# Three mixed pairs of contraction tiles in ten gate/up units of each layer, in another order, with the residual in DRAM meanwhile

## The chip, the cores and the metric

One core of one Trainium2 chip runs the whole program. The metric is the device time of one execution in microseconds. The program is built from instructions for five engines, each with its own in-order queue: TensorE (PE) multiplies, VectorE (DVE) and ScalarE (ACT) work elementwise, GpSimd (POOL) and SyncE (SP) here mostly issue transfers and small steps. Semaphores order them.

## The reference

256 tokens of width 2048 pass two layers: a Mamba-2 layer, then a sliding-window attention layer. Each has a SwiGLU feed-forward part, and around every part stands an RMS norm on both sides. The change concerns the feed-forward part alone:

```python
D_MODEL, SEQ, DEPTH = 2048, 256, 2
D_FF = 5632

def swiglu(u, w_gate, w_up, w_down):
    return (jax.nn.silu(u @ w_gate) * (u @ w_up)) @ w_down

for layer in range(DEPTH):
    g = norm_w[layer]
    mix = mamba2_mixer(...) if layer == 0 else sliding_window_sink_attention(...)
    h = h + rmsnorm(mix, g[1])
    ffn = swiglu(rmsnorm(h, g[2]), ffn_w_gate[layer], ffn_w_up[layer], ffn_w_down[layer])
    h = h + rmsnorm(ffn, g[3])
```

All data are float32.

## The kernel before

**Products.** A float32 product is made of three matmuls in a rounded format: high half by high half, high by low, low by high. ScalarE casts a weight tile to its high half (`whi`, L114), VectorE subtracts that from the weight for the low half (`wlo`, L115). The activations `xh`, `xl` are split once per part. The contraction of 2048 is cut into 16 tiles of 128, and the class `Weights` walks through the weights of the whole program in a fixed list of specs.

**Weight rings.** A raw tile is 128 x 1024 float32: two contraction tiles of 512 columns, 512 KB, one transfer on SP's queue (L70). There are `RAWB` = 5 raw buffers. A sub-tile is what is converted at once; there are `CVB` = 4 buffers each for `whi` and `wlo`, so the conversion of a sub-tile waits for TensorE to be through with the fourth one before it. Loads run four raw tiles ahead, conversions three sub-tiles.

**Units.** The gate and up products of a layer run over 11 units of 512 columns. A *plain* unit takes 8 sub-tiles of gate (`G0` to `G7` below) and 8 of up (`U0` to `U7`), each of two contraction tiles: 2 token halves x 2 tiles x 3 = 12 matmuls of 128 x 512, 192 in the unit. In a *mixed* unit some pairs (e, o) of contraction tiles are multiplied for gate and up together by seven products in place of eight: the 2 x 2 scheme has the token halves and the two contraction tiles on one side, and gate and up of both tiles on the other. Such a pair takes two raw tiles, `ta` = gate(e), up(o) and `tb` = gate(o), up(e), each loaded by two transfers of 256 KB, and four sub-tiles, named "a" (`ta` itself), "13" (sums of `ta` and up(e), L87), "24" (two more sums, L90 and L91, each of 128 x 512) and "g" (gate(o) alone, 128 x 512). The seven products make 21 matmuls in place of 24. The matching sums of the activations, `sx`, are made once a layer by `mixed_x`. The products are summed over all pairs in seven banks p1 to p7 and one more, `up1`; behind the last pair and at the end of the unit VectorE puts them together (L700 to L703, L708), ScalarE applies silu, and VectorE multiplies gate and up (L712). `store_half` transposes a half of the previous unit's result on TensorE (4 transposes, L644) and splits it into `hh` and `hl` (L237 on ScalarE, L238 on VectorE).

Before the change units 1 to 8 are mixed, with `SPAIRS` = 2 pairs each (186 matmuls); units 0, 9 and 10 are plain. `S_ORDER` is [0, 2, 1, 3, 4, 5, 6, 7]: numbers below `SPAIRS` are mixed pairs, the others are plain pairs of contraction tiles, gate then up. The two store halves stand after positions 5 and 6.

**What sets the order.** The instructions are issued in program order on each engine, with a scheduler that moves what the code marks as urgent. So VectorE's queue holds the low halves, the sums of weights, the sums of banks and the splitting of the stores in one fixed order, and each waits behind the one ahead of it.

**Space.** `h`, the residual, is 128 x 2 x 2048 float32 in SBUF for the whole program (L469 on). In the feed-forward part `hh` and `hl` of units 0 to 7 lie in one pair of tiles, and those of units 8 to 10 in another (`Cat`, `late`) that takes the place of `sx`, `vh`, `t13` and `t24` when the mixed units are over.

**Entry.** In unit 0, `a_first` updates `h` by the mixer's result chunk by chunk (L533) while it makes the gate product. Then `row_factor` takes the norm's row factors from `h` (L223, L224, and a power on POOL, L228), and `mixed_x` is called between the sub-tiles of up 0.

Of the kernel before, what the change touches and what calls it, by code (L numbers as in the profile page):

```python
# [14 lines left out]
P = 128  # L15
# [15 lines left out]
SPAIRS = 2  # L31
S_FIRST, S_LAST = 1, 8
LATE = 8


class Weights:
# [40 lines left out]
    def _mixed(self, i, part):  # L77
# [11 lines left out]
        t24 = self.spool.tile([P, 2, CW], F32, tag="t24", name="t24")  # L89
        nc.vector.tensor_tensor(t24[:, 0, :], self.t13[:, 0, :], ta[:, 1, :], add)  # L90
        nc.vector.tensor_tensor(t24[:, 1, :], t24[:, 0, :], tb[:, 0, :], add)  # L91
        return t24[:]
# [42 lines left out]
def tile_yoco(ctx: ExitStack, tc: tile.TileContext, a: dict):  # L135
# [11 lines left out]

    rest = list(range(SPAIRS, KD // SUB))
    S_ORDER = [i for n in range(SPAIRS) for i in ([n] + rest[n : n + 1])][: 2 * SPAIRS - 1] + rest[SPAIRS - 1 :]
    S_END = S_ORDER.index(SPAIRS - 1)  # L150

# [320 lines left out]
    h = hpool.tile([P, NT, D], F32, tag="h", name="h")  # L472
    for t in range(NT):
        nc.sync.dma_start(h[:, t, :], x[P * t : P * (t + 1), :])
# [55 lines left out]
    def add_residual(mix, t, c):  # L530
        bks, rs = mix
        hs = h[:, t, CW * c : CW * (c + 1)]
        nc.vector.scalar_tensor_tensor(hs, bks[c][t][:], rs[t][:, 0:1], hs, ALU.mult, ALU.add)  # L533

    def a_first(key, mix, g, xt):
# [11 lines left out]
        def step(c, t):  # L547
            with tc.high_priority():
                update(c, t)
                to_xt(h[:, t, CW * c : CW * (c + 1)], t, c, g, xt)  # L550
# [24 lines left out]
    def row_factor():  # L575

        return [norm_stats(hpool, h, t) for t in range(NT)]
# [17 lines left out]
    class Cat:  # L595


        def __init__(self, n, early, late):
            self.n, self.tiles = n, (early, late)

        def at(self, k0, k1, ts):
            t = k0 >= self.n
            return self.tiles[t][:, k0 - self.n * t : k1 - self.n * t, ts]

        def __getitem__(self, idx):
            _, kt, ts = idx
            return self.at(kt, kt + 1, ts)[:, 0, :]

    def ffn(layer, mix):
        xt = new_xt()  # L610
        xh, xl, _ = xt
        with tc.tile_pool(name="ffn%d" % layer, bufs=1, side="right") as fp:
            early = [fp.tile([P, 4 * LATE, T], F32R, tag=n, name=n) for n in ("hh", "hl")]
            spool = tc.tile_pool(name="mixed%d" % layer, bufs=1, side="right")
            W.spool = sp = spool.__enter__()
            sx = sp.tile([P, SPAIRS, 4, 2, P], F32R, tag="sx", name="sx")
            vh = sp.tile([P, 2, CW], F32, tag="vh", name="vh")
            hid = None
# [9 lines left out]
            def mixed_x(i):  # L628


                y = sp.tile([P, 2, T], F32, tag="sy", name="sy")
                ks = slice(SUB * i, SUB * i + 2)
                nc.vector.tensor_tensor(y[:], xh[:, ks, :].bitcast(F32), xl[:, ks, :].bitcast(F32), ALU.add)
                e0, e1, o0, o1 = y[:, 0, :P], y[:, 0, P:], y[:, 1, :P], y[:, 1, P:]
                f = sp.tile([P, 4, P], F32, tag="sf", name="sf")
                for n, p, q in ((1, e1, o1), (3, e0, e1), (2, e0, f[:, 1, :]), (0, o0, f[:, 2, :])):
                    nc.vector.tensor_tensor(f[:, n, :], p, q, ALU.subtract)
                split_bank(sx[:, i, :, 0, :], sx[:, i, :, 1, :], f[:])

            def store_half(u, t):  # L640

                pt = bank()
                for k in range(4):
                    nc.tensor.transpose(pt[:, P * k : P * (k + 1)], scr[:, NT + t, P * k : P * (k + 1)], ident[:])  # L644
                ts = slice(P * t, P * (t + 1))
                split_bank(hid[0].at(4 * u, 4 * u + 4, ts), hid[1].at(4 * u, 4 * u + 4, ts),
                           pt[:].rearrange("p (k t) -> p k t", k=4))
# [5 lines left out]
            def mixed_unit(u):  # L653
# [28 lines left out]
                for pos, i in enumerate(S_ORDER):  # L682
                    e, o = SUB * i, SUB * i + 1
                    if i < SPAIRS:
                        for part, prods in (("a", (("p1", raw_x(e, 0)), ("p3", form(i, 0)))),
                                            ("13", (("p5", form(i, 1)), ("p7", form(i, 3)))),
                                            ("24", (("p6", form(i, 2)), ("p4", raw_x(o, 1)))),
# [16 lines left out]
                    if pos in (5, 6):  # L704
                        store_half(u - 1, pos - 5)
# [10 lines left out]
            for u in range(FF // CW):  # L716
                if S_FIRST <= u <= S_LAST:
                    if u == S_FIRST:
                        hid = [Cat(4 * LATE, e, None) for e in early]
                    mixed_unit(u)  # L720
                    if u == S_LAST:
                        spool.__exit__(None, None, None)
                        lpool = tc.tile_pool(name="late%d" % layer, bufs=1, side="right")
# [523 lines left out]
```

## Time and profile before

| | us |
|---|---|
| median of 3 runs | 2410.99 |
| lowest, highest run | 2410.32, 2412.8 |
| profiled execution, its own time | 2411.38 |
| its span | 2409.7 |
| TensorE busy | 2390.0 |
| TensorE weight loads busy | 1980.7 |
| VectorE busy | 1667.9 |
| ScalarE busy | 1279.7 |
| GpSimd busy | 87.2 |

The profiled execution's time is the span and 1.7 us around it. The mean granted clock is 0.998. Busy times are unions of what the profiler saw of an engine. In a timeline a row gives the start, the duration, engine, line and operation, what is written and read with its shape, and in brackets the idle time ahead of it with what ended it. TensorE's matmuls are pipelined, so the duration of one is longer than its distance from the next. In a table of windows the columns behind the stretch are its length, then for PE, weight loads, DVE, ACT and POOL the busy time with the count, then the granted clock, the share of the DMA engines and GB/s.

### The profile page before, as it was taken

Reading aid. Unit: us, or ns where it says so; the run is one execution under the profiler, and the core shown is the slowest. Engines: PE = TensorE matmul, PEld = TensorE weight load, DVE = VectorE, ACT = ScalarE, POOL = GpSimd, SP = SyncE. Lnnn points to the kernel's source line nnn. Section 1 sums busy time; section 2 is a strip of 40 time slices with the busy share of each in tenths; the row PEclk is TensorE's granted clock in tenths of the full one; section 3 lists DMA queues with packets and bytes.
Section 4 is the critical chain, followed back from the end, with each engine's and each line's share of the span. In section 5 each row is a group of like instructions: output and inputs, shape, how many; then the busy total and the mean of one; then the engine's idle time right before and its main releaser. Section 6 shows DMA issues by size and latency. Waiting matters only on the chain.

```text
span 2409.7 us, 31424 instructions
## 1 busy us (share of the span) xinstructions
PE 2390.0 (99%) x11714; PEld 1980.7 (82%) x11714; DVE 1667.9 (69%) x2329; ACT 1279.7 (53%) x1805; POOL 87.2 (4%) x66
## 2 busy tenths in 40 slices
PE   9999999999999999999999999999999999999998
PEld 8888888888878888888888878777888888888887
DVE  6998878875577878875444468865878778554444
ACT  6566766654464545544444457755545555444443
POOL 2500100000000000000000000000000000000000
PEclk9999999999999999999999999999999999999999
DMA  7666666657656565666666664445665656666664
GB/s 223 184 202 192 186 190 191 183 178 244 193 165 200 177 216 168 216 201 185 207 193 194 194 191 153 128 126 163 191 202 177 214 177 199 201 189 207 194 194 143
DMA packets 285434, 453.80 MB, mean 188 GB/s; under 512 B 18000, under 2 KB 116560, under 8 KB 284512
## 3 DMA queue, kind: packets, MB, share of 16 engines
q1 hardware_dynamic: 284960, 451.39, 60.9%
q8 instruction: 92, 1.51, 0.3%
q14 instruction: 62, 0.51, 0.1%
q10 hardware_dynamic: 288, 0.33, 0.0%
q0 software_dynamic: 32, 0.07, 0.0%
HBM read 449.56 MB, written 2.16 MB: 187 GB/s over the span
## 4 chain that ended last, share of the span: by engine, by line
PE 97%; ACT 1%; DVE 1%; issue 0%; POOL 0%; DVEq 0%; POOLq 0%; ACTq 0%
PE bank L291 14%; PE bank L350 14%; PE bank L351 14%; PE bank L349 14%; PE bank L672 9%; PE bank L673 9%; PE bank L671 9%; PE bank L296 7%; PE bank L644 1%; PE bank L949 1%; PE bank L1125 1%; PE bank L1168 1%; DVE wlo L115 1%; PE bank L411 1%; ACT xx L270 0%; PE bank L1160 0%
## 5 line engine op out<-in xcount | busy, mean ns | idle before, releaser
L115 DVE TENSOR_TENSOR wlo<-raw,whi 128x1024 fp32r<-128x1024 f32 (+1 forms) x785 | 936.1, 1200 | 568.8 <-ACT whi L114 567.6
L114 ACT CAST whi<-raw 128x1024 fp32r<-128x1024 f32 (+1 forms) x785 | 811.1, 1036 | 828.9 <-PE bank L351 506.3
L291 PE MATMUL bank<-xx,whi 128*128 128x512 f32 (+1 forms) x1488 | 523.3, 396 | 0.0
L296 PE MATMUL bank<-xx,wlo 128*128 128x256 f32 (+1 forms) x1488 | 416.1, 285 | 0.0
L672 PE MATMUL bank<-wlo,xx 128*128 128x512 f32 x864 | 336.9, 390 | 0.3 <-DVE wlo L115 0.2
L671 PE MATMUL bank<-whi,xx 128*128 128x512 f32 x864 | 337.2, 393 | 0.0
L673 PE MATMUL bank<-whi,xx 128*128 128x512 f32 x864 | 336.9, 390 | 0.0
L291 PEld LDWEIGHTS bank<-xx,whi 128*128 128x128 f32 (+1 forms) x1488 | 276.6, 188 | 61.2 <-issue 0.4
L296 PEld LDWEIGHTS bank<-xx,wlo 128*128 128x128 f32 (+1 forms) x1488 | 280.2, 188 | 11.4 <-issue 7.0
L349 PE MATMUL bank<-whi,hh 128*128 128x512 f32 x512 | 199.3, 389 | 0.0
L351 PE MATMUL bank<-whi,hl 128*128 128x512 f32 x512 | 199.2, 389 | 0.0
L350 PE MATMUL bank<-wlo,hh 128*128 128x512 f32 x512 | 199.2, 389 | 0.0
L672 PEld LDWEIGHTS bank<-wlo,xx 128*128 128x128 f32 x864 | 162.3, 188 | 35.2 <-DVE wlo L115 2.1
L673 PEld LDWEIGHTS bank<-whi,xx 128*128 128x128 f32 x864 | 162.2, 188 | 34.2
L671 PEld LDWEIGHTS bank<-whi,xx 128*128 128x128 f32 x864 | 162.2, 188 | 32.8
L349 PE MATMUL bank<-whi,xx 128*128 128x512 f32 x416 | 162.6, 393 | 2.5 <-ACT xx L270 2.1
L351 PE MATMUL bank<-whi,xx 128*128 128x512 f32 x416 | 162.5, 392 | 0.9 <-DVE xx L271 0.9
L350 PE MATMUL bank<-wlo,xx 128*128 128x512 f32 x416 | 162.3, 391 | 0.5 <-DVE wlo L115 0.5
L114 ACT CAST whi<-t 128x1024 fp32r<-128x1024 f32 x64 | 67.2, 1050 | 107.7 <-DVE t L91 49.8
L351 PEld LDWEIGHTS bank<-whi,hl 128*128 128x128 f32 x512 | 96.1, 188 | 20.1
L350 PEld LDWEIGHTS bank<-wlo,hh 128*128 128x128 f32 x512 | 96.1, 188 | 20.0
L349 PEld LDWEIGHTS bank<-whi,hh 128*128 128x128 f32 x512 | 96.1, 188 | 19.7
(222 smaller groups left out, 3157.4 us busy)
## 6 DMA issues: line engine op xcount, KB each, us to landing
raw<-in_ffn_w_down_dram SPq DMA_DIRECT2D x176, 512.0 KB, 4.9
raw<-in_ssm_w_in_dram SPq DMA_DIRECT2D x161, 512.0 KB, 4.6
raw<-in_ffn_w_gate_dram SPq DMA_DIRECT2D x144, 512.0 KB, 4.5
raw<-in_ffn_w_up_dram SPq DMA_DIRECT2D x144, 512.0 KB, 4.6
raw<-in_ssm_w_out_dram SPq DMA_DIRECT2D x64, 512.0 KB, 4.8
raw<-in_ffn_w_gate_dram SPq DMA_DIRECT2D x64, 256.0 KB, 3.2
raw<-in_ffn_w_up_dram SPq DMA_DIRECT2D x64, 256.0 KB, 3.7
raw<-in_attn_w_q_dram SPq DMA_DIRECT2D x32, 512.0 KB, 3.4
```

The lines of the kernel that those rows point to most:

```text
L114: self.pin(nc.scalar.copy(hi[:], src))
L115: self.pin(nc.vector.tensor_tensor(lo[:], src, hi[:].bitcast(F32), ALU.subtract))
L291: nc.tensor.matmul(o, wh, xx[:, kt, :, :].rearrange("p a t -> p (a t)"), start=(kt == 0), stop=(kt == kts - 1))
L296: nc.tensor.matmul(o[:, :T], wl, xx[:, kt, 0, :], start=False, stop=False)
L349: nc.tensor.matmul(o, sh, wh, start=(kt == 0), stop=False)
L350: nc.tensor.matmul(o, sh, wl, start=False, stop=False)
L351: nc.tensor.matmul(o, sl, wh, start=False, stop=(kt == kts - 1))
L411: nc.tensor.matmul(o[:], hi[:, kk, cs], xr[2][:, kt, :, :].rearrange("p a t -> p (a t)"), start=(kt == 0), stop=(kt == KD - 1))
L644: nc.tensor.transpose(pt[:, P * k : P * (k + 1)], scr[:, NT + t, P * k : P * (k + 1)], ident[:])
L671: nc.tensor.matmul(o, sh, wh, start=(n == 1), stop=False)
L672: nc.tensor.matmul(o, sh, wl, start=False, stop=False)
L673: nc.tensor.matmul(o, sl, wh, start=False, stop=(n == total[name]))
```

## The change

Five things go together. `SPAIRS` is 3, so three of the eight pairs of contraction tiles are mixed. Units 1 to 10 are mixed; only unit 0 stays plain. `S_ORDER` is [3, 0, 4, 1, 5, 2, 6, 7]: a unit opens with a plain pair, the last mixed pair stands at position 5, and the stores follow positions 6 and 7, so the second one comes behind the unit's last product. The 24-combination is written in place into `ta`, whose buffer is therefore held until its low half is made; products of "24" change places (p4, then p6). And `h` leaves SBUF: after gate 0 and the row factors two transfers of 1 MB on POOL's queue write it to DRAM, `sx`, `vh` and `t13` take its place, and after unit 10 two transfers bring it back. `hh` and `hl` are one pair of tiles for all units, and `mixed_x` uses `t13`'s buffer for its intermediates.

```diff
-SPAIRS = 2
-S_FIRST, S_LAST = 1, 8
-LATE = 8
+SPAIRS = 3
+S_ORDER = [3, 0, 4, 1, 5, 2, 6, 7]
+S_END = S_ORDER.index(SPAIRS - 1)
...
-        t24 = self.spool.tile([P, 2, CW], F32, tag="t24", name="t24")
-        nc.vector.tensor_tensor(t24[:, 0, :], self.t13[:, 0, :], ta[:, 1, :], add)
-        nc.vector.tensor_tensor(t24[:, 1, :], t24[:, 0, :], tb[:, 0, :], add)
-        return t24[:]
+        nc.vector.tensor_tensor(ta[:, 1, :], self.t13[:, 0, :], ta[:, 1, :], add)
+        nc.vector.tensor_tensor(ta[:, 0, :], ta[:, 1, :], tb[:, 0, :], add)
+        return ta[:]
...
-            if not S_FIRST <= u <= S_LAST:
+            if u == 0:
...
-    h = hpool.tile([P, NT, D], F32, tag="h", name="h")
+    hd = dram.tile([P, NT, D], F32, tag="hd", name="hd")
+    h = []
+
+    def open_h():
+        pool = tc.tile_pool(name="hres", bufs=1)
+        h[:] = [pool, pool.__enter__().tile([P, NT, D], F32, tag="h", name="h")]
+        return h[1]
+
+    def spill_h():
+        for t in range(NT):
+            nc.gpsimd.dma_start(hd[:, t, :], h[1][:, t, :])
+        h[0].__exit__(None, None, None)
+
+    def fetch_h():
+        ht = open_h()
+        for t in range(NT):
+            nc.gpsimd.dma_start(ht[:, t, :], hd[:, t, :])
...
             def mixed_x(i):
-                y = sp.tile([P, 2, T], F32, tag="sy", name="sy")
+                t = sp.tile([P, 2, CW], F32, tag="t13", name="yf")
...
-                                            ("24", (("p6", form(i, 2)), ("p4", raw_x(o, 1)))),
+                                            ("24", (("p4", raw_x(o, 1)), ("p6", form(i, 2)))),
...
-                    if pos in (5, 6):
-                        store_half(u - 1, pos - 5)
+                    if pos > S_END:
+                        store_half(u - 1, pos - S_END - 1)
...
+                gb = a_first("gate%d_%d" % (layer, u), mix, gt[:, layer, 2, :], xt)
+                rs = row_factor()
+                spill_h()
+                sp = spool.__enter__()
+                W.spool = sp
+                sx = sp.tile([P, SPAIRS, 4, 2, P], F32R, tag="sx", name="sx")
+                vh = sp.tile([P, 2, CW], F32, tag="vh", name="vh")
...
+            spool.__exit__(None, None, None)
+            fetch_h()
+            todo += [None, lambda: store(FF // CW - 1)]
```

**The boundary of two units on VectorE.** Here is its queue before the change, from the last low halves of a mixed unit to the opening of the next one; `raw` and `t` are the weights and their sums, L238 is a store half, L708 the last sums of banks, L712 the product of gate and up.

```order
L115 TENSOR_TENSOR wlo<-raw,whi 128x1024
L115 TENSOR_TENSOR wlo<-t_7938,whi 128x1024
L238 TENSOR_TENSOR hl<-bank,hh 128x4x128
L708 TENSOR_TENSOR scr<-bank,scr 128x512 x2
L87 TENSOR_TENSOR t_8037<-raw 128x1024
L115 TENSOR_TENSOR wlo<-t_7958,whi 128x1024
L708 TENSOR_TENSOR vh<-bank,vh 128x512 x2
L712 SCALAR_TENSOR_TENSOR scr<-vh,rs,scr 128x512 x2
L115 TENSOR_TENSOR wlo<-raw,whi 128x512
```

The low halves of "13" and "24" of the next unit's first pair stand here, with their sums made long before (the sum `t_7958` is older than this stretch). After the change the same place of VectorE's queue reads so; line numbers have moved (L114 is the low half, L233 a store half, L697 to L700 and L705 the sums of banks, L709 the product, L89 and L90 the two sums of "24"):

```order
L114 TENSOR_TENSOR wlo<-raw,whi 128x1024
L233 TENSOR_TENSOR hl<-bank,hh 128x4x128
L705 TENSOR_TENSOR scr<-bank,scr 128x512 x2
L87 TENSOR_TENSOR t_8022<-raw 128x1024
L114 TENSOR_TENSOR wlo<-raw,whi 128x1024
L705 TENSOR_TENSOR vh<-bank,vh 128x512 x2
L233 TENSOR_TENSOR hl<-bank,hh 128x4x128
L709 SCALAR_TENSOR_TENSOR scr<-vh,rs,scr 128x512 x2
L114 TENSOR_TENSOR wlo<-t_8022,whi 128x1024
L89 TENSOR_TENSOR raw<-t_8022,raw 128x512
L90 TENSOR_TENSOR raw<-raw 128x512
L114 TENSOR_TENSOR wlo<-raw,whi 128x1024
```

The first row is `U3'`, the up half of the next unit's opening plain pair (a prime marks the next unit), the fifth is its `a0'`, the ninth `13_0'` and the last `24_0'`. Both sums of "24" and its low half have moved behind the whole end of the unit, and the second store half stands between the sums of banks and the product.

**The pairs behind it on VectorE.** The rest of the same unit, from the low half of its first "24" to the low half of its third, after the change:

```order
L114 TENSOR_TENSOR wlo<-raw,whi 128x512
L114 TENSOR_TENSOR wlo<-raw,whi 128x1024 x3
L87 TENSOR_TENSOR t_8113<-raw 128x1024
L89 TENSOR_TENSOR raw<-t_8113,raw 128x512
L90 TENSOR_TENSOR raw<-raw 128x512
L114 TENSOR_TENSOR wlo<-t_8113,whi 128x1024
L114 TENSOR_TENSOR wlo<-raw,whi 128x1024
L114 TENSOR_TENSOR wlo<-raw,whi 128x512
L114 TENSOR_TENSOR wlo<-raw,whi 128x1024 x2
L87 TENSOR_TENSOR t_8196<-raw 128x1024
L114 TENSOR_TENSOR wlo<-raw,whi 128x1024
```

The three low halves in the second row are `G4`, `U4` and `a1`; then come the sums of the second pair, each reading a raw tile that has been loaded into a buffer freed by the "24" before it: the load of `tb1` waits for the low half of `24_0`, that of `tb2` for the low half of `24_1`, and that of `U7` for the low half of `24_2`.

**POOL.** Its queue around the feed-forward part of layer 0 holds the mixer's row factors (L240), the spill (L478), the norm's row factors (L223), the fetch (L484) and then the next part's; after the change:

```order
L240 TENSOR_TENSOR rs<-ms,neghalf 128x1 x2
L478 DMA hd<-h 128x2048 x2
L223 TENSOR_TENSOR rs<-ms,neghalf 128x1 x2
L484 DMA h<-hd 128x2048 x2
L240 TENSOR_TENSOR rs<-ms,neghalf 128x1
```

Before, the rows of L478 and L484 were not there. The row factors of the silu now stand behind the spill, and the first row factor of the down projection behind the fetch. On VectorE the first add of `mixed_x` (L631) waits for both spill transfers, since `t13` lies where `h` lay.

More of the change, by code (lines that the diff above doesn't have):

```diff
@@ L575, in row_factor @@
     def row_factor():
-        return [norm_stats(hpool, h, t) for t in range(NT)]
+        return [norm_stats(hpool, h[1], t) for t in range(NT)]
     def to_row(rs):
@@ L593, in by_row @@
                                 rr[:].unsqueeze(1).broadcast_to([P, 2, T]), ALU.mult)
[L595 to L607, printed above, removed]
     def ffn(layer, mix):
@@ L716, in ffn @@
             for u in range(FF // CW):
[L717 to L719 removed]
+                if u:
                     mixed_unit(u)
[L721 to L735 removed]
+                    continue
+                gb = a_first("gate%d_%d" % (layer, u), mix, gt[:, layer, 2, :], xt)
[5 more added lines that the diff above has]
+                vh = sp.tile([P, 2, CW], F32, tag="vh", name="vh")
+                for i in range(SPAIRS):
+                    todo += [None, lambda i=i: mixed_x(i)]
                 for t in range(NT):
```

48 lines of the change are left out of this document (15 added, 33 removed).

## The prediction

> **What bounds the kernel now.** I read the page first, from the span down to the chain that ended last.
>
> ```profile
> span 2409.7 us, 31424 instructions
> ...
> PE 2390.0 (99%) x11714; PEld 1980.7 (82%) x11714; DVE 1667.9 (69%) x2329; ACT 1279.7 (53%) x1805; POOL 87.2 (4%) x66
> ...
> PE 97%; ACT 1%; DVE 1%; issue 0%; POOL 0%; DVEq 0%; POOLq 0%; ACTq 0%
> ...
> L672 PE MATMUL bank<-wlo,xx 128*128 128x512 f32 x864 | 336.9, 390 | 0.3 <-DVE wlo L115 0.2
> ```
>
> TensorE is 97% of the chain, and the 864 products with a low half in the mixed units waited 0.3 us in all. So a matmul that goes is worth its whole slot, as long as the weights keep arriving. What one slot is, two neighbouring rows of TensorE's timeline show:
>
> ```profile
> 871.65 0.39 PE L673 MATMUL bank<-whi,xx 128*128 128x512 f32 x1
> 871.88 0.39 PE L671 MATMUL bank<-whi,xx 128*128 128x512 f32 x1
> ```
>
> 0.39 is the pipelined duration; the slot is the distance of starts, 0.2275 over several rows. Next I took the period of a unit, for a plain one from the chain in order of time (the eight transposes of its store), for a mixed one from ScalarE's copy of p1:
>
> ```profile
> 1093.26 0.87 PE bank L644 x8
> 1137.71 0.87 PE bank L644 x8
> ```
>
> ```profile
> 839.98 0.58 ACT L699 COPY scr<-bank 128x512 f32<-128x512 f32 x1
> ...
> 883.15 0.58 ACT L699 COPY scr<-bank 128x512 f32<-128x512 f32 x1
> ```
>
> 44.45 and 43.17. A plain unit has 192 matmuls and a mixed one 186: 192 x 0.2275 + 0.87 = 44.55 and 186 x 0.2275 + 0.87 = 43.19. The counts explain both, so mixed units run without stalls today. The question is VectorE, whose busy time is the third figure of the row of one mixed unit in the windows:
>
> ```profile
> 836.00:880.00 44.00, 44.00 (x199) 36.41 (x198) 35.36 (x39) 22.58 (x25) 0.00 (x0) 1.00 0.62 197
> ```
>
> 35.4 of 44.0 us, 80%. This is the engine that the change loads.
>
> **The change part by part: matmuls.** A third mixed pair replaces 24 matmuls by 21, so a unit goes from 186 to 183 in sixteen units (48 fewer), and from 192 to 183 in the four units 9 and 10 (36 fewer). 84 x 0.2275 = **-19.1 us**. Unit period without stall: 183 x 0.2275 + 0.87 = 42.5.
>
> The Trainium skill, "TensorE: Matmul & The Clock Gate", section "Wait — 56ns, not 53.3ns?", gives 215.7 ns start to start for 512 columns in the warm state. The rows above show 227.5 with the granted clock at 1.00, so by the page the gain would be 18.1, an estimate, and the measurement decides.
>
> **The opening of unit 1.** There the trace has a late weight:
>
> ```profile
> 746.66 0.39 PE L671 MATMUL bank<-whi,xx 128*128 128x512 f32 x1
> 747.25 0.50 PE L672 MATMUL bank<-wlo,xx 128*128 128x512 f32 x1 [0.20 <-DVE wlo L115]
> 747.58 0.39 PE L673 MATMUL bank<-whi,xx 128*128 128x512 f32 x1
> ```
>
> ```profile
> 745.97 1.22 DVE L115 TENSOR_TENSOR wlo<-raw,whi 128x1024 fp32r<-128x1024 f32 x1
> ```
>
> Two slots took 0.92 in place of 0.455: 0.46 lost. It also gives the rule that I use below: the low half ended at 747.19, 0.53 after the start of its sub-tile's first matmul, and cost 0.465, so lateness is that end less the start, less 0.065. After the change the unit opens with a plain pair and this stall should go; the code is the same in both layers: **-0.9**.
>
> **What VectorE gets.** In a third pair two plain low halves go, three mixed ones of 1024 and one of 512 come, with an add of 1024 and two of 512. Over the program I count 56 more operations of 1024 and 118 more of 512. Their price, from the boundary of two units:
>
> ```profile
> 868.42 0.68 DVE L238 TENSOR_TENSOR hl<-bank,hh 128x512 fp32r<-128x512 f32 x1
> 869.02 1.28 DVE L708 TENSOR_TENSOR scr<-bank,scr 128x512 f32<-128x512 f32 x2
> 870.22 1.21 DVE L87 TENSOR_TENSOR t<-raw 128x1024 f32<-128x1024 f32 x1
> 871.35 1.22 DVE L115 TENSOR_TENSOR wlo<-t,whi 128x1024 fp32r<-128x1024 f32 x1
> 872.49 1.28 DVE L708 TENSOR_TENSOR vh<-bank,vh 128x512 f32<-128x512 f32 x2
> 873.69 1.40 DVE L712 SCALAR_TENSOR_TENSOR scr<-vh,rs,scr 128x512 f32<-128x512 f32 x2
> ```
>
> By starts: 1.13 for 1024, 0.60 for 512, 1.32 for the two products of L712. 56 x 1.13 + 118 x 0.60 = 134 us. What hides it is VectorE's idle time: today 0.80 x 43.2 = 34.7 of a unit is busy, the new pair adds 2 x 1.13 + 3 x 0.60 = 4.1, so some 38.9 of 42.5, 91% (units 9 and 10 get more, and end at the same figure). So the sum holds only if no single weight comes late, and that takes the order.
>
> **The boundary.** The order of after puts, behind the last low half that is plain (U3'): both stores, four sums L705, the first pair's 13-add, the low halves of a0' and 13_0', the two products, and then the two adds of the 24-combination. Set t = 0 at the end of U7. The plain sub-tiles take 12 slots = 2.73, a store half 0.44; PE then reaches 24_0' at 0.44 + 5.46 + 2.73 = 8.63. What a cast waits for:
>
> ```profile
> 865.73 0.39 PE L673 MATMUL bank<-whi,xx 128*128 128x512 f32 x1
> ```
>
> ```profile
> 866.20 1.05 ACT L114 CAST whi<-t 128x1024 fp32r<-128x1024 f32 x1 [1.71 <-PE bank L673]
> ```
>
> The slot ended at 865.96, the cast began 0.24 later. Four slots: the cast of U3' waits for U6, which ends at -5.90; cast -5.65 to -4.60, low half from -4.57. From there VectorE runs without a gap: 1.13 (U3'), 0.60 (store), 1.20 (L705), 1.13 (13-add), 1.14 (a0'), 1.20 (L705), 0.60 (store), 1.32 (products), 1.14 (13_0'): the adds begin at 4.89. Behind them, as before:
>
> ```profile
> 880.15 0.69 DVE L90 TENSOR_TENSOR t<-t,raw 128x512 f32<-128x512 f32 x1
> 880.87 0.69 DVE L91 TENSOR_TENSOR t<-t,raw 128x512 f32<-128x512 f32 x1
> 882.76 1.23 DVE L115 TENSOR_TENSOR wlo<-t,whi 128x1024 fp32r<-128x1024 f32 x1 [1.19 <-ACT whi L114]
> ```
>
> ```profile
> 881.68 1.05 ACT L114 CAST whi<-t 128x1024 fp32r<-128x1024 f32 x1 [3.50 <-DVE t L91]
> ```
>
> 0.72 + 0.69 + 0.12 + 1.05 + 0.03 + 1.23: the low half of 24_0' ends at 8.73 against 8.63 + 0.065. That is 0.035 late, on the edge. Without error it costs 20 x 0.035 = 0.7; with the ledger's pitches off by 0.2 it costs nothing or 0.24 a unit, 5. I take **+1.5**, nearest to the sum. The cover, if gone, is worth one microsecond a unit for each microsecond that VectorE is later.
>
> **The raw buffers.** The 24-combination is now written into the raw tile of a pair, which is freed only by that low half, so tb1 waits for 24_0', tb2 for 24_1, U7 for 24_2. What a load of a pair takes:
>
> ```profile
> 897.94 0.42 SPq L70 DMA_DIRECT2D raw<-in_ffn_w_up_dram  x1
> ```
>
> ```profile
> 902.18 1.22 DVE L87 TENSOR_TENSOR t<-raw 128x1024 f32<-128x1024 f32 x1 [1.93 <-DMA raw<-in_ffn_w_up_dram]
> ```
>
> ```profile
> raw<-in_ffn_w_gate_dram SPq DMA_DIRECT2D x1, 256.0 KB, 3.1
> raw<-in_ffn_w_up_dram SPq DMA_DIRECT2D x1, 256.0 KB, 3.3
> ```
>
> ```profile
> raw<-in_ffn_w_gate_dram SPq DMA_DIRECT2D x144, 512.0 KB, 4.5
> ...
> raw<-in_ffn_w_gate_dram SPq DMA_DIRECT2D x64, 256.0 KB, 3.2
> raw<-in_ffn_w_up_dram SPq DMA_DIRECT2D x64, 256.0 KB, 3.7
> ```
>
> The first is 4.1 with the trains of 512 KB loads ahead of it, the two of the window at 908.9, behind a quiet stretch, 3.1 and 3.3. In the new order the pairs' loads come behind a quiet stretch (VectorE works on 13 and 24, which free nothing), so I take L = 3.1 to 3.3. The loop of VectorE and buffers for one unit, with an issue 0.41 behind the freeing low half and 0.14 to the waiting add: from 24_0' to 24_1 max(4.0, L + 0.55) + 4.9, to 24_2 L + 0.55 + 7.4, to the next 24_0' 22.0 of VectorE's work (seven low halves and four sums to the end of U3', 9.8, and the 12.2 of the boundary above). The 4.0 is VectorE's own work in between, 0.61 + 3 x 1.13; 4.9 and 7.4 are the adds, cast and low halves up to the next 24, by the same prices. At L = 3.1 this is 42.0, below TensorE's 42.5; at 3.5 it is 42.4. So **0** for the buffers, with 0.1 to 0.5 us a unit of room: thin.
>
> **The spill.** Residual h goes out by two 1 MB transfers on POOL's queue after its last update in gate 0, and the first add of mixed_x waits for both, since its buffer lies where h lay. Rows of VectorE in layer 0, before:
>
> ```profile
> 704.39 0.74 DVE L533 SCALAR_TENSOR_TENSOR h<-bank,rs,h 128x512 f32<-128x512 f32 x1
> ...
> 713.73 0.68 DVE L633 TENSOR_TENSOR sy<-xx 128x512 f32<-128x512 f32 x1
> ...
> 714.63 1.22 DVE L115 TENSOR_TENSOR wlo<-raw,whi 128x1024 fp32r<-128x1024 f32 x1
> ```
>
> ```profile
> 717.68 0.69 ACT L737 ACTIVATE scr<-bank,rs 128x512 f32<-128x512 f32 x1 [1.68 <-PE bank L351]
> ```
>
> Behind the add stand the low halves of up 0 and the row factor of the silu, on POOL the rows of the same factor. Gate 0 ended just before 717.68, and TensorE needs the low half of 714.63 one sub-tile later, at about 720.2: the add may start 4.4 late, 13 us after the last update, for nothing. Nearest rows for a transfer of this size, and for one on POOL's queue:
>
> ```profile
> h<-in_x_dram SPq DMA_DIRECT2D x2, 1024.0 KB, 8.7
> ...
> cumd<-scr POOLq DMA_DIRECT2D x1, 64.0 KB, 4.4
> ```
>
> 8.7 hides (705.1 + 8.7 = 713.8); sixteen times 4.4 = 70 would block some 55 us a layer. 1 MB in large rows is nearer to the first: **0**. The fetch after unit 10 is needed a whole down projection later: 0.
>
> The Trainium skill, "DMA: Bandwidth & Descriptors", section "Anatomy of one DMA — SWDGE (gpsimd) path", prices such a transfer at 2.0 us + bytes / 436e3, an estimate of 4.4 for 1 MB; by it the spill is hidden too, and no run of before shows one.
>
> **Sum:** -19.1 - 0.9 + 1.5 = -18.5 on the profiled execution's 2411.38 (0.4 above the median of the runs, 2410.99): **2393.0**.
>
> **The rivals.** *First, small stalls at the edge.* Each unit loses 0.3 to 0.7 because VectorE's chain at the boundary, or a tb2 that lands at 3.7, is a little later than my ledger: 20 x 0.3 to 0.7 = 6 to 14, so 2398 to 2406. For it speaks 91% on an in-order engine, against it that before's boundary shows no stall at 80%.
>
> *Second, and slower: the loop of raw buffers becomes the bound.* The point is the landing of a pair. With M = L + 0.5 for U7's 512 KB, whose low half comes 5.2 behind 24_2, the loop is 35.4 + 2 L + max(0, L - 3.5). It equals the mean unit of before (16 x 43.17 and 4 x 44.45 make 43.4) at L = 3.85. At the 4.1 of the row above it is 44.2: 20 x 0.8 = 16 slower, 2427; between 3.85 and 4.3, 2411 to 2438. For it speaks the page's median of 3.7 for the later half; against it the quiet stretch ahead of the loads, and that data rates stay near 197 GB/s.
>
> *Third, the spill blocks VectorE:* each microsecond past 13 costs one per layer. 20 us a layer makes 2407, 55 us 2500. The Trainium skill, "SBUF — State Buffer", section "Who interferes with whom", says that a transfer issued by GpSimd can be held up while VectorE runs copies or casts in its two-port modes, but not by tensor_tensor; the rows above are tensor_tensor and scalar_tensor_tensor, so by that rule nothing holds the spill.
>
> *Fourth, the change is not what it says:* the counts come from the built program, so I give this nothing apart.
>
> **How the numbers follow.** Forecast (2389 to 2398) 0.60; first rival (2398 to 2406) 0.19; a mixture of both that ends near no change (2406 to 2416) 0.08; second rival beyond it 0.09; third beyond it 0.04. A change of 0.2%, 4.8 us, is about what a measurement of this kernel can tell from none. Faster 0.79, same 0.08, slower 0.13. The range reaches from 2388 (no stall at all, 2391, less the 0.1% by which runs differ) to 2411.
>
> **What would show it.** 8940 matmuls of 512 in place of 9024; copies of p1 42.5 apart: right. If they are 42.8 to 43.2 apart with low halves of 24_0' as releaser of idle TensorE, the boundary is the failed step; if VectorE's 13-add waits for a transfer in every unit, the buffers are; if the first add of mixed_x starts after 718, the spill is. What makes it wrong most easily is a VectorE operation 0.3 slower with operands in place than these rows show, six times in a unit.

## The result, and the profile after

| | before | after |
|---|---|---|
| median | 2411.68 (4 runs, 2410.32 to 2412.8) | 2395.26 (4 runs, 2393.57 to 2396.51) |
| profiled execution | 2411.38 | 2395.28 |
| its span | 2409.7 | 2393.6 |
| TensorE, VectorE busy | 2390.0, 1667.9 | 2371.8, 1808.4 |
| matmuls on TensorE | 11714 | 11630 |

The ratio is 0.9932 with a 95% interval of 0.9917 to 0.9947: 16.4 us less. The prediction was 2393.0. From the page of the changed kernel (line numbers moved by one to five: L668 to L670 are now the matmuls of the mixed units, L114 the low half, L113 the cast):

```profile
span 2393.6 us, 31662 instructions
...
PE 2371.8 (99%) x11630; PEld 1963.9 (82%) x11630; DVE 1808.4 (76%) x2513; ACT 1322.2 (55%) x1867; POOL 92.0 (4%) x74
...
PE 95%; ACT 2%; DVE 2%; issue 1%; DMA 0%; POOL 0%; DVEq 0%; SPq 0%; ACTq 0%; POOLq 0%
...
L668 PE MATMUL bank<-whi,xx 128*128 128x512 f32 x980 | 385.2, 393 | 0.5 <-ACT whi L113 0.5
L669 PE MATMUL bank<-wlo,xx 128*128 128x512 f32 x980 | 382.2, 390 | 1.8 <-DVE wlo L114 1.8
```

TensorE still carries the chain, but no longer alone: the low halves of the mixed units made it wait 1.8 us and the casts 0.5, where it was 0.3 and nothing. ScalarE's copies of p1 give the units:

```profile
981.44 0.58 ACT L696 COPY scr<-bank 128x512 f32<-128x512 f32 x1
...
1023.95 0.58 ACT L696 COPY scr<-bank 128x512 f32<-128x512 f32 x1
...
1066.44 0.58 ACT L696 COPY scr<-bank 128x512 f32<-128x512 f32 x1
...
1110.16 0.57 ACT L696 COPY scr<-bank 128x512 f32<-128x512 f32 x1
```

42.51, 42.49, and then 43.72. (The copy itself was also held up in the last one; what TensorE lost there is 0.77, at the late matmul and the one behind it.) Adding up the distances of TensorE's matmuls beyond a slot in both layers, I find four places: 0.77 in unit 9 of layer 0, 0.23 in unit 1, 0.81 in unit 7 and 1.78 in unit 9 of layer 1, **3.6 us** in all. Sixteen of the twenty units run without a stall. VectorE in one of them, in the row of a window from copy to copy:

```profile
981.44:1023.95 42.51, 42.51 (x193) 35.06 (x192) 38.86 (x44) 24.00 (x29) 0.00 (x0) 1.00 0.59 198
```

38.86 of 42.51 us, the 91% that was forecast.

**A late unit.** VectorE waits for the second transfer of tb2, and 7 us later TensorE waits for the low half of 24_2:

```profile
1103.59 1.23 DVE L87 TENSOR_TENSOR t<-raw 128x1024 f32<-128x1024 f32 x1 [1.12 <-DMA raw<-in_ffn_w_up_dram]
```

```profile
1111.04 0.50 PE L669 MATMUL bank<-wlo,xx 128*128 128x512 f32 x1 [0.50 <-DVE wlo L114]
```

What moved in the DMA engines at that time (window 1099 to 1103.7), and in the unit before, which did not stall (1056.5 to 1061; the last figure is the time to landing):

```profile
q8 instruction: 1, 0.02, 1.2%
...
raw<-in_ffn_w_up_dram SPq DMA_DIRECT2D x1, 256.0 KB, 4.4
```

```profile
raw<-in_ffn_w_up_dram SPq DMA_DIRECT2D x1, 256.0 KB, 3.0
```

The second window has no transfer of q8, the queue that the profile calls instruction. I went through all twenty loads of tb2. Without a q8 transfer beside it the later half landed in 2.9 to 3.4 us, fourteen times. With one it took 2.9, 3.0 and 3.2, and 4.3, 4.4 and 4.9 in just the three units that lost most. In the first three the transfer began 2.7 to 2.9 us behind the issue, with the load all but landed; in the late ones 1.8 to 2.4 us behind it. The page has 91 such transfers of 1.49 MB (before: 92). TensorE's 11630 matmuls and as many weight loads, divided by 91, are 256 instructions a transfer, so by the counts it is TensorE's own code.

The load of tb0, the first pair's, runs beside loads of 512 KB, and it shows the same in more cases. Here is its later half in unit 7 of layer 0, with a q8 transfer (window 987.4 to 990), and in unit 6, without one (944.9 to 947.5):

```profile
q8 instruction: 1, 0.02, 2.4%
...
raw<-in_ffn_w_up_dram SPq DMA_DIRECT2D x1, 256.0 KB, 5.9
```

```profile
raw<-in_ffn_w_up_dram SPq DMA_DIRECT2D x1, 256.0 KB, 4.6
```

In units 2 to 10 of both layers a q8 transfer falls on eight of these loads, all in odd units. They land in 5.0 to 6.4 us, the ten others in 4.0 to 4.8 (means 5.56 and 4.39). TensorE lost nothing by them in this kernel: tb0 has more room than tb2.

**The spill** behaves as priced. POOL issues the second half at the last update of h; it lands 4.6 us later, and VectorE reaches the add of mixed_x at 713.38 without waiting:

```profile
705.08 0.54 POOL L478 DMA_DIRECT2D hd<-h  x1 [11.02 <-DVE xx L266]
```

```profile
hd<-h POOLq DMA_DIRECT2D x1, 1024.0 KB, 4.6
```

```profile
713.38 0.68 DVE L631 TENSOR_TENSOR yf<-xx 128x512 f32<-128x512 f32 x1
```

The Trainium skill, "DMA: Bandwidth & Descriptors", section "Anatomy of one DMA — SWDGE (gpsimd) path", made this an estimate of 4.4: the four spill transfers took 4.2 to 4.7, so the trace agrees, while the two of a fetch, issued 0.6 us apart, took 5.5 and 8.0.

### The profile page after: what moved, and what is told of

It reads as the page before. It is cut to its first block, busy times and chain, and to the rows that moved or that the text cites. A ratio compares the mean times of both kernels' runs of the same rounds, so it can differ in the third digit from the quotient of the medians.

```text
span 2393.6 us, 31662 instructions
## 1 busy us (share of the span) xinstructions
PE 2371.8 (99%) x11630; PEld 1963.9 (82%) x11630; DVE 1808.4 (76%) x2513; ACT 1322.2 (55%) x1867; POOL 92.0 (4%) x74
## 3 DMA queue, kind: packets, MB, share of 16 engines
q8 instruction: 91, 1.49, 0.3%
## 4 chain that ended last, share of the span: by engine, by line
PE 95%; ACT 2%; DVE 2%; issue 1%; DMA 0%; POOL 0%; DVEq 0%; SPq 0%; ACTq 0%; POOLq 0%
PE bank L286 14%; PE bank L345 12%; PE bank L346 12%; PE bank L344 12%; PE bank L669 11%; PE bank L670 11%; PE bank L668 11%; PE bank L291 8%; PE bank L641 1%; ACT whi L113 1%; DVE wlo L114 1%; PE bank L940 1%; PE bank L1116 1%; PE bank L1159 1%; PE bank L406 1%
## 5 line engine op out<-in xcount | busy, mean ns | idle before, releaser
L114 DVE TENSOR_TENSOR wlo<-raw,whi 128x1024 fp32r<-128x1024 f32 (+1 forms) x845 | 988.6, 1184 | 471.5 <-ACT whi L113 465.0
L113 ACT CAST whi<-raw 128x1024 fp32r<-128x1024 f32 (+1 forms) x845 | 853.7, 1022 | 790.4 <-PE bank L346 413.8
L668 PE MATMUL bank<-whi,xx 128*128 128x512 f32 x980 | 385.2, 393 | 0.5 <-ACT whi L113 0.5
L669 PE MATMUL bank<-wlo,xx 128*128 128x512 f32 x980 | 382.2, 390 | 1.8 <-DVE wlo L114 1.8
L670 PE MATMUL bank<-whi,xx 128*128 128x512 f32 x980 | 382.3, 390 | 0.0
L344 PE MATMUL bank<-whi,hh 128*128 128x512 f32 x704 | 274.2, 390 | 0.0
L346 PE MATMUL bank<-whi,hl 128*128 128x512 f32 x704 | 274.0, 389 | 0.0
L345 PE MATMUL bank<-wlo,hh 128*128 128x512 f32 x704 | 273.9, 389 | 0.0
L668 PEld LDWEIGHTS bank<-whi,xx 128*128 128x128 f32 x980 | 184.1, 188 | 38.1 <-ACT whi L113 0.9
L670 PEld LDWEIGHTS bank<-whi,xx 128*128 128x128 f32 x980 | 184.0, 188 | 37.9
L113 ACT CAST whi<-t 128x1024 fp32r<-128x1024 f32 x60 | 63.2, 1054 | 90.6 <-DVE t L87 73.9
L344 PE MATMUL bank<-whi,yh 128*128 128x512 f32 x256 | 100.1, 391 | 0.0
L346 PE MATMUL bank<-whi,yl 128*128 128x512 f32 x256 | 99.7, 390 | 0.0
L345 PE MATMUL bank<-wlo,yh 128*128 128x512 f32 x256 | 99.6, 389 | 0.0
```

The costliest lines, as they stand in the source:

```text
L113: self.pin(nc.scalar.copy(hi[:], src))
L114: self.pin(nc.vector.tensor_tensor(lo[:], src, hi[:].bitcast(F32), ALU.subtract))
L344: nc.tensor.matmul(o, sh, wh, start=(kt == 0), stop=False)
L345: nc.tensor.matmul(o, sh, wl, start=False, stop=False)
L346: nc.tensor.matmul(o, sl, wh, start=False, stop=(kt == kts - 1))
L668: nc.tensor.matmul(o, sh, wh, start=(n == 1), stop=False)
```

## The experiments

The theory to be tested: the 84 matmul slots set the gain; VectorE's chain at the boundary and the load of tb2 are the two places with almost no room, and tb2's late landings are what the forecast missed. Rivals are given with each run. "Stall" means TensorE's lost time, summed as above.

**1. Two pairs in ten units.** The part of the change that mixes units 9 and 10, with the old pairs and order; spill, fetch and in-place sums stay.

```diff
-SPAIRS = 3
-S_ORDER = [3, 0, 4, 1, 5, 2, 6, 7]
+SPAIRS = 2
+S_ORDER = [0, 2, 1, 3, 4, 5, 6, 7]
+S_STORE = (5, 6)
```

> Units 1 to 10 mixed, with the two pairs and the order of before; spill, fetch and the in-place 24 as in the changed kernel. Theory, matmul slots: 186 in place of 192 in four units, 24 x 0.2275 = 5.5 less than before, the opening stall of unit 1 stays: 2406 (+-1.5), units 43.17 apart. Rival, spill, fetch or the in-place sums cost something of their own: 2409 or above.

2405.38 (2404.26 to 2406.72), ratio 0.9975 (0.9965 to 0.9984): 5.9 less than before's 2411.29, units 43.13 to 43.14 apart, no stall. The slots explain it; spill, fetch and in-place sums have no price to be seen. The opening stall of unit 1 is gone too, which I had expected to stay. The rest of the gain, some 10 us, belongs to the third pair and its order.

**2. An order in the old style with three pairs.**

```diff
-S_ORDER = [3, 0, 4, 1, 5, 2, 6, 7]
+S_ORDER = [0, 3, 1, 4, 2, 5, 6, 7]
+S_STORE = (5, 6)
```

> Three pairs in ten units as in the changed kernel, in an order in the style of before: 0, 3, 1, 4, 2, 5, 6, 7, stores after the sixth and seventh position. Theory, matmul slots set the time and the order only moves stalls: between 24_1 and 24_2 TensorE has the same work, so tb2 has the same thin room; the late weight at the opening of unit 1 (0.46 a layer) comes back: 2395 to 2397. Rival, the new order is what carries three pairs: the boundary or the pairs stall in every unit by 0.3 us or more, 2401 or above.

2391.67 (2391.62 to 2391.89), ratio 0.9918 (0.9905 to 0.9932). Better than either forecast: no stall anywhere in the units, which are 42.45 apart. This is what the slots give alone: on the same chip it is 13.7 less than two pairs in run 1, and three slots of 0.2275 in each of twenty units are 13.65. Half of the reason stands in VectorE's queue at the third pair:

```profile
1059.39 1.22 DVE L115 TENSOR_TENSOR wlo<-t,whi 128x1024 fp32r<-128x1024 f32 x1
1060.67 1.83 DVE L115 TENSOR_TENSOR wlo<-raw,whi 128x1024 fp32r<-128x1024 f32 x2
```

```profile
1063.20 0.39 PE L669 MATMUL bank<-whi,xx 128*128 128x512 f32 x1
```

Here the low half of 13_2 stands behind both sums of 24_2 and fills the time of the cast, so 24_2's low half ends at 1061.9 against a need at 1063.2 and 0.065: 1.4 us of room, where the changed kernel has 0.4. The other half: in this kernel's trace no code transfer of q8 falls on a load of tb0, tb1 or tb2 at all. This run does not part the two.

**3. The 13-add of the third pair twice.**

```diff
             nc.vector.tensor_tensor(self.t13[:], ta[:], tb[:, 1:2, :].broadcast_to([P, 2, CW]), add)
+            self.n13 = getattr(self, "n13", 0) + 1
+            if self.n13 % SPAIRS == 0:
+                nc.vector.tensor_tensor(self.t13[:], ta[:], tb[:, 1:2, :].broadcast_to([P, 2, CW]), add)
```

> The changed kernel with the 13-add of the third pair of every unit made twice (same result, 1.13 us more of VectorE between the landing of tb2 and the low half of 24_2). Theory, the chain from 24_1 over the load of tb2 to 24_2 has 0.3 to 0.45 us of room a unit: it stalls TensorE by 0.7 us in every unit, 20 x 0.7 = 14 more than the changed kernel, 2408 to 2412. Rival, what counts is VectorE's idle share (9% of a unit, 3.6 us): 1.13 us are absorbed, 2395 to 2398.

2395.81 (2393.62 to 2397.7): nothing. The rival's time came out, though not by its reason. The added row made the scheduler move the low half of 13_2 (here 1066.44) behind the sums:

```profile
1063.86 1.22 DVE L90 TENSOR_TENSOR t<-raw 128x1024 f32<-128x1024 f32 x1
1065.11 0.69 DVE L92 TENSOR_TENSOR raw<-t,raw 128x512 f32<-128x512 f32 x1
1065.83 0.69 DVE L93 TENSOR_TENSOR raw<-raw 128x512 f32<-128x512 f32 x1
1066.44 1.22 DVE L117 TENSOR_TENSOR wlo<-t,whi 128x1024 fp32r<-128x1024 f32 x1
1067.73 3.18 DVE L117 TENSOR_TENSOR wlo<-raw,whi 128x1024 fp32r<-128x1024 f32 x3
```

In the changed kernel VectorE idles 1.19 us between the second sum and that last low half, for the cast. The added 1.13 went into this gap: the low halves of 24_1 and 24_2 end 11.28 us apart in place of 10.99. So the run added 0.3 us to the chain and not 1.13, which the 0.44 of room takes. As a test of that room it is void. Its trace has two late units, 5 and 9 of layer 1, where tb2 landed in 4.5 and 5.0 us with a code transfer beside it.

**4. A buffer of its own for 24.** Three small buffers were moved or made single to find 4 KB a partition.

```diff
-        nc.vector.tensor_tensor(ta[:, 1, :], self.t13[:, 0, :], ta[:, 1, :], add)
-        nc.vector.tensor_tensor(ta[:, 0, :], ta[:, 1, :], tb[:, 0, :], add)
-        return ta[:]
+        t24 = self.spool.tile([P, 2, CW], F32, tag="t24", name="t24")
+        nc.vector.tensor_tensor(t24[:, 1, :], self.t13[:, 0, :], ta[:, 1, :], add)
+        nc.vector.tensor_tensor(t24[:, 0, :], t24[:, 1, :], tb[:, 0, :], add)
+        return t24[:]
```

> Both sums of 24 get a buffer of their own again; all else is as in the changed kernel (three small buffers are moved or made single to find the space). Theory, the load of tb2 is late because its raw buffer is held by 24_1 until that low half is made: the load starts about 3 us earlier, the three late units of the changed kernel's profile (0.77, 0.81 and 1.78 us of idle TensorE) go, all 20 units have a period of 42.5, and the time is 2395.3 - 3.6 = 2391.7. Rival, the late landings come from the 512 KB loads beside them whatever buffer they use: stalls of the same sum somewhere in the units, 2394 to 2397.

2403.53 (2400.76 to 2406.71), ratio 0.9968 (0.9955 to 0.998): 8 us slower than with the sums in place, against both expectations. With the freed buffers VectorE's order is another one: the 13-add of the next unit's first pair moved ahead of the last plain low half and the bank sums, where its transfer has not landed, and everything behind it waits with it. In layer 0 this makes the low half of 24_0' late in every second unit, in layer 1 in most:

```profile
995.50 1.23 DVE L87 TENSOR_TENSOR t<-raw 128x1024 f32<-128x1024 f32 x1 [1.56 <-DMA raw<-in_ffn_w_up_dram]
```

```profile
1007.58 1.22 DVE L115 TENSOR_TENSOR wlo<-t,whi 128x1024 fp32r<-128x1024 f32 x1 [1.20 <-ACT whi L114]
```

```profile
1008.86 0.50 PE L670 MATMUL bank<-wlo,xx 128*128 128x512 f32 x1 [0.76 <-DVE wlo L115]
```

All stalls of this run make 9.8 us, all but two of them at this place; the two are at 24_2 of unit 1, whose tb2 landed in 4.3 and 4.5 us here without a code transfer. That it is every second unit in layer 0 comes from the code transfer again. In units 3, 5, 7 and 9 it falls on tb0, which lands in 4.5 to 5.4 us; in the even units it does not, and tb0 lands in 3.6 to 4.0. Unit 7 (window 990.2 to 993):

```profile
q8 instruction: 1, 0.02, 2.2%
...
raw<-in_ffn_w_up_dram SPq DMA_DIRECT2D x1, 256.0 KB, 5.2
```

So the run shows the boundary's lack of room, not the buffer's: whether the raw buffer held by 24 is what makes tb2 fragile was not settled by this run.

**5. Shifting the code transfers.** Two units of the changed kernel are 764 instructions on TensorE, nearly three transfers of 256, so a transfer that meets tb2 in one unit meets it again two units later. The eight transposes of the first store are repeated, which shifts them against the units of both layers.

```diff
-                for k in range(4):
+                for k in list(range(4)) * (3 if (layer, u) == (0, 0) else 1):
```

> The changed kernel with the eight transposes of unit 0's store in layer 0 made three times: 32 more instructions on TensorE (16 transposes and their weight loads), 16 x 0.11 = 1.8 us of its time. In the changed kernel's trace the three late tb2 all have a transfer of TensorE's own code beside them (91 transfers, 256 instructions each; two units have 764 instructions, so the transfers keep their place in the units, one of them at tb2 of every second unit). Theory, the collision with the code transfer makes tb2 late: 32 instructions move it 3.5 us ahead, before the load is issued; no tb2 lands later than 3.5 us, the stalls go, and the time is 2395.3 + 1.8 - 3.6 = 2393.5. Rival, late landings are hazards of the memory: stalls of 2 to 5 us remain at tb2, 2396 to 2399.

> The same transposes nine times: 128 more instructions, 64 x 0.11 = 7 us of TensorE's time. Theory of the code transfers: they move by half a transfer, 14 us ahead, which is where the tb2 of the other units lie (28.3 us from one transfer to the next against a unit of 42.5), so late tb2 come back, now in the even units (2, 4, 6, 8, 10) and no longer in the odd ones; 2395.3 + 7 = 2402.3, +-1.5. Rival, hazards of the memory: late tb2 in any units, without such a rule, the same time.

With 32 more instructions: 2396.18 (2395.57 to 2396.89). No q8 transfer begins within a load of tb2 any more. Nineteen of the twenty land in 2.9 to 3.4 us, one in 3.6, beside a transfer of the other instruction queue, q14. No 24_2 stalls by more than 0.2; two small stalls at a boundary remain, at 24_0 of unit 3 and, in layer 1, of unit 2, 0.9 us together. But the time did not fall to 2393.5, and two readings say why. The profiled run reaches the last row factor ahead of the part (POOL, L240) at 694.04, where the changed kernel's first profile has 692.58. The changed kernel's second profile, that of experiment 8, has 694.01, so this 1.5 us is a difference between executions of the same code. And that second profile (2395.73) lost 2.8 us in stalls, not 3.6. Against it this run (2396.0) loses 1.0, so it saves 1.8, and it pays 1.8 for the transposes: 1.4 more in layer 0, where they stand, and 1.4 less in layer 1. In place the theory held; in the total the saving only paid for its own price.

With 128 more: 2401.8 (2401.43 to 2404.09), as expected. The q8 transfer now meets tb2 in units 6, 8 and 10 of layer 0 and 4, 6, 8 and 10 of layer 1, where it met 7 and 9, and 3, 5, 7 and 9. The stalls over 0.2 are in unit 8 (0.81), and in units 6 and 10 of layer 1 (1.15, 1.09): even units only. Unit 8:

```profile
q8 instruction: 1, 0.02, 1.2%
...
raw<-in_ffn_w_up_dram SPq DMA_DIRECT2D x1, 256.0 KB, 4.3
```

```profile
1068.98 1.22 DVE L87 TENSOR_TENSOR t<-raw 128x1024 f32<-128x1024 f32 x1 [1.16 <-DMA raw<-in_ffn_w_up_dram]
```

The loads of tb0 turned round too. A q8 transfer now falls on nine of the eighteen, all in even units, and these land in 5.0 to 5.9 us, the nine others in 3.9 to 4.6 (means 5.44 and 4.27).

So the late landings go with the code transfers, not with chance, and in both kernels one costs a load of tb0 some 1.2 us. For tb2, in this order, it also counts when the transfer begins. In four traces of it (two of the changed kernel, that of experiment 3 and this one) 23 loads of tb2 met one, and the 57 others landed in 2.8 to 3.4 us. Of the 23, all seven whose transfer began in the first 2.1 us of the load were late (3.9 to 5.0 us), four of the ten between 2.2 and 2.6, and none of the six behind that (3.6 at most). In other orders tb2 can be late without one: in experiment 6 it landed in 3.7 to 5.2 us where none was beside it.

**6. A boundary with less room.** The third pair later, both stores at the end, and, as the queue then stands, the second store half and all bank sums ahead of the next 13-add.

```diff
-S_ORDER = [3, 0, 4, 1, 5, 2, 6, 7]
+S_ORDER = [3, 0, 4, 1, 5, 6, 2, 7]
+S_STORE = (6, 7)
```

> Order 3, 0, 4, 1, 5, 6, 2, 7 with the stores after the last two positions: the third pair stands later, and the second store half and all sums of the unit stand ahead of the first pair's 13-add on VectorE. Theory, the ledger of the boundary: the low half of 24_0' ends at 10.1 us behind the end of U7 and TensorE needs it at 8.7, 1.4 us of stall in each of the nine boundaries of a layer, 25 in all; tb2 has room. 2391.5 + 25 = 2413 to 2419. Rival, the boundary has more room than the ledger says (the changed kernel shows no stall there though it was worked out as 0.035 late): 2391 to 2400.

2417.94 (2417.19 to 2419.43), ratio 1.0029 (1.0018 to 1.0039): slower than before the change. TensorE's waits:

```profile
PE bank L669 <- ACT whi L114: 13.2, 18, 0.7
```

Eighteen times, once in each boundary of units 2 to 10 in both layers. What a boundary costs is seen in the copies of p1:

```profile
994.17 0.59 ACT L697 COPY scr<-bank 128x512 f32<-128x512 f32 x1
```

```profile
1038.07 0.59 ACT L697 COPY scr<-bank 128x512 f32<-128x512 f32 x1
```

The units are 43.90 apart where the changed kernel has 42.50: 1.4 a boundary, as the ledger has it, and 25 for eighteen. So the ledger is right in size. In place it is one step off: TensorE's own queue has another order here, with three products of high halves of 13_0' and 24_0' ahead of those of low halves, so TensorE waits for the cast of 24_0' (and 0.3 for that of 13_0' before it), where the ledger names the low half behind it.

**7. Four pairs**, VectorE doing all of it, and then with the 13-adds on GpSimd.

```diff
-SPAIRS = 3
-S_ORDER = [3, 0, 4, 1, 5, 2, 6, 7]
+SPAIRS = 4
+S_ORDER = [0, 4, 1, 5, 2, 6, 3, 7]
+S_STORE = (1, 2)
```

> Four mixed pairs in ten units, order 0, 4, 1, 5, 2, 6, 3, 7, stores after the second and third position. Theory, VectorE becomes the bound: its work is 38.9 + 4.1 = 43.0 us a unit and it waits for casts at least 1.2 more, against 41.8 of TensorE: 44.2 or more a unit, 2425 or more. Rival, TensorE still sets the time: 12 slots fewer in four units... 3 matmuls fewer in each of 20 units, 13.7 us less than three pairs without stalls, 2378 to 2385.

2447.3 (2447.13 to 2447.48), ratio 1.0149 (1.0128 to 1.0169). VectorE is busy 42.46 of 46 us in this window, about one unit (they are 45.3 to 46.8 apart), and more than the 41.8 that TensorE would need for a unit:

```profile
1014.00:1060.00 46.00, 42.95 (x186) 33.80 (x187) 42.46 (x48) 24.57 (x29) 0.00 (x0) 1.00 0.55 183
```

TensorE waits in all units, for casts, low halves and sums in turn. With a fourth pair, in the one order that was run, VectorE's work passes TensorE's: 14 us fewer of matmuls than with three pairs, and a loss of 36 against the kernel before.

```diff
-            nc.vector.tensor_tensor(self.t13[:], ta[:], tb[:, 1:2, :].broadcast_to([P, 2, CW]), add)
+            nc.gpsimd.tensor_tensor(self.t13[:], ta[:], tb[:, 1:2, :].broadcast_to([P, 2, CW]), add)
```

> Four mixed pairs as in the run with four pairs, with the 13-add of every pair on GpSimd in place of VectorE. Theory, VectorE was the bound there (2447.3): 4 x 1.13 = 4.5 us a unit leave it, it has 38.5 of 41.8 us to do, the share of the changed kernel; GpSimd's add of 128x512 took 1.27 us in the last step of the changed kernel, so 2.5 for each of four 13-adds, 10 us a unit. If GpSimd runs beside VectorE without slowing it: some stalls where the longer add is waited for, 2380 to 2400. Rival, the two engines hinder each other (adds far over 2.5 us, or VectorE's 128x1024 over 1.25 us): 2410 or above.

2603.55 (2600.5 to 2606.31), ratio 1.0792 (1.0774 to 1.081). The rival's side, and further than it said:

```profile
L88 POOL TENSOR_TENSOR t<-raw 128x1024 f32<-128x1024 f32 x80 | 263.0, 3287 | 815.9 <-DMA raw<-in_ffn_w_up_dram 691.5 <-ACT whi L114 82.4 <-DVE wlo L115 25.9
```

```profile
1004.11 2.04 DVE L115 TENSOR_TENSOR wlo<-raw,whi 128x1024 fp32r<-128x1024 f32 x1 [0.39 <-ACT whi L114]
```

```profile
1000.00:1046.00 46.00, 42.68 (x164) 32.58 (x163) 35.80 (x39) 20.96 (x24) 14.41 (x4) 0.89 0.52 171
```

An add takes 3.29 us on GpSimd in the mean, from 2.37 to 5.27, and a low half beside one (it ran from 1002.16 to 1005.07) took 2.04 in place of 1.22. Not every such meeting costs VectorE time: of the 131 low halves of 128x1024 that overlap an add, 30 took 1.85 to 3.42 us, and all of these start during the add and end behind it; the 101 others kept their 1.22, and it is the adds beside them that are long (the longest, 5.27, has three). VectorE is busy 35.8 of 46 us, less than in the run before, so it waits more, and TensorE, busy for 42.68, was granted 0.89 of its clock in this window. The Trainium skill, "SBUF — State Buffer", section "Who interferes with whom", says that a VectorE operation with two SBUF inputs contends with a GpSimd operation that reads SBUF; the trace agrees. How the 192 us of loss divide over slower operations, waits and clock was not taken apart.

**8. The two best once more, on one chip.**

> The changed kernel once more, on the same chip as the next run. Theory: 2395.3, and its runs spread over 2 to 3 us, since how many tb2 are late depends on where a code transfer falls to a microsecond.

> The kernel with the order 0, 3, 1, 4, 2, 5, 6, 7 once more, beside the changed one. Theory: tb2 has 1.9 us of room there, a late landing of up to 1.9 us is hidden, so no stall in any run: 2391.7, runs within 0.5 us, 3 to 4 us below the changed kernel. Rival: the difference of the first measurement was one of chips or of chance, below 1.5 us.

2394.58 (2393.44 to 2395.73) and 2391.37 (2391.01 to 2391.8). The ranges don't meet, the difference is 3.2 us, and the order 0, 3, 1, 4, 2, 5, 6, 7 beats both kernels, 0.9919 of before (0.9906 to 0.9933). The changed kernel shows stalls again in unit 9 and, in layer 1, in units 1, 7, 8 and 9, 2.8 us; the other none. The pair confirms the difference and not its reason. The room is the 1.4 of run 2 and not the 1.9 expected, and again no code transfer falls on a tb2 of this order (they land in 2.9 to 3.4 us), so no run shows what a late landing would do to it.

## Why the prediction was right, by its own steps

- **Matmuls, -19.1.** Right; 84 matmuls went and a unit without stall takes 42.50. Measured against 8 x 43.17 + 2 x 44.45 a layer, ten such units are 9.3 less, so -18.5: a plain unit was 44.45 and not 44.55. Runs 1 and 2 show the slot's price apart from the stalls: 24 slots and the opening stall, 5.5 + 0.9, gave 5.9, and 60 slots more, 13.65, gave 13.7.
- **Opening of unit 1, -0.9.** The stall is gone in the changed kernel, in layer 0 wholly; in layer 1 unit 1 lost 0.23 elsewhere. But the reason given, the plain pair at the start, is not the one: the runs that open with a mixed pair (1, 2) don't have it either. Before, the second pair's 13-add stood ahead of that late low half and waited for a transfer:

```profile
741.17 1.23 DVE L87 TENSOR_TENSOR t<-raw 128x1024 f32<-128x1024 f32 x1 [2.16 <-DMA raw<-in_ffn_w_up_dram]
```

  In run 1 that low half runs at 744.36 and the add behind it, at 745.50. So it is VectorE's order again by these two traces; no run was made to isolate it.
- **Boundary, +1.5.** Nothing was lost there in the first profile, and 0.2 in the second. The ledger had the low half of 24_0' 0.035 late; the trace has it just in time, at 1047.28 for a sub-tile begun at 1047.21, which the 0.065 allows:

```profile
1047.21 0.39 PE L668 MATMUL bank<-whi,xx 128*128 128x512 f32 x1
```

```profile
1046.05 1.23 DVE L114 TENSOR_TENSOR wlo<-raw,whi 128x1024 fp32r<-128x1024 f32 x1 [1.19 <-ACT whi L113]
```

  Experiment 6 shows that the step's price was right, and its place but for one step.
- **Raw buffers, 0.** This term was mis-sized: 3.6 us came from it, 3.4 of them from a tb2 that landed at 4.3 to 4.9. L = 3.1 holds for the usual unit and its room of 0.44 is the ledger's (0.1 to 0.5). What failed is the step from "a quiet stretch" to one value of L: the queue of weights was quiet, the code transfers were not thought of. It is the first rival's second mechanism, a late tb2, in three units in place of twenty; the 0.23 of a fourth came with a tb2 that landed in 3.0.
- **Spill, 0.** Right, with 4.6 us for the later half; run 1, which has the spill too, shows no price either.
- **Sum.** -18.5 - 0.9 + 3.6 = -15.8 against the -16.1 of the two profiled executions. That 2393.0 lay so near owes something to terms that cancel: +1.5 stood for a stall that was not there, 0 for one that was, and how large that one is depends on where the code transfers fall (2.8 in the second profile).
- **The slower rivals.** The loop of raw buffers did not become the bound, but experiments 6 and 7 show both of its neighbours: a pair more, or a boundary 1.4 us later, and the kernel is slower than before.

## What to carry to other kernels

When one engine is at its slot rate, count its instructions for the gain, and then look for the loss in the in-order engine that feeds it: not its share of busy time, but the latest chain per unit with its room in microseconds. A room of half a microsecond is spent by the tail of a transfer's landing, so price loads by their tail. Something independent (a low half, in run 2) in the wait of a cast gives room, though these runs do not show that it is what took the stalls away. When a list scheduler sets the order, read the resulting order after each edit: two of these edits (3 and 4) changed it and thereby measured something else than they were meant to.

## What was not expected of the hardware

The code of an engine comes by DMA, in transfers of 256 of TensorE's instructions here, and shares the engines with the weights. Where one fell on a 256 KB load that usually lands in 3.0 us, the load took 3.9 to 5.0 in about half of the cases, and always when it began in the first 2.1 us of the load. On a 256 KB load beside 512 KB ones it cost some 1.2 us each time (5.0 to 6.4 against 3.9 to 4.8). Since a unit is a nearly fixed number of instructions, the collisions come back every second unit, and 128 added instructions moved them from the odd to the even ones. So transfers of 16 KB, with 0.3% of the DMA engines' time in all, made most of the changed kernel's stalls.
